# Slab pairs that take expert weights to the end, instead of turning into gather and result buffers

## The chip, the cores and the metric

The program runs on one core of a Trainium2 chip. The metric is device time in microseconds, the median of three runs. Beside it stands one profiled execution of the same program, whose rows carry all durations below.

## The reference

One transformer block on 1024 tokens of width 1024, in float32: a first half (projections, two kinds of attention, gates, an output projection) and a mixture of 32 experts, which is the stage that the change touches:

```
for e in range(N_EXPERTS):
    hidden = jax.nn.silu(t @ w_gate[e]) * (t @ w_up[e])
    out = out + combine[:, e:e + 1] * (hidden @ w_down[e]).astype(jnp.float32)
```

Each token goes to two of the 32 experts (the top two in its best group); `combine` is zero elsewhere. So 2048 token rows are computed in all, and the kernel gathers for each expert the rows that chose it, up to `BT` = 112 at a time.

## The kernel before, in words

The first 880 us or so are the block's first half and the router; the change leaves them alone. Then comes the stage of the experts, one expert after the other, e = 0 to 31.

An expert's weights are six slabs of 128x1024 floats (512 KB each): j = 0 to 3 hold gate and up, j = 4 and 5 hold down. A slab is loaded by SyncE (L870), then `split` (L82 to L84) makes two tiles of it for TensorE: ScalarE writes the rounded part `ehi`, VectorE writes the rest, `elo`. After both have read it, the slab is free and its next load may land. `weights(e, j0, j1)` (L1111) does this for a run of slabs and asks for the next loads in the order of `raw_order` (L860): expert by expert, j by j.

The raw slabs are 24 in number when the stage starts: five `er`, three `ex`, and 16 halves of eight pairs called `ring` (L125). The pairs held other things before (the input, then the merged branches) and are loaded with weights as they come free, while the router runs (`load_pairs`, L873). So experts 0 to 3 are in SBUF when the stage begins.

For each expert: `gather(e)` (L1129) fetches its token rows from the DRAM tensor `h2_d` by an indirect DMA that GpSimd issues; `tokens(e)` (L1135) turns them with eight TensorE transposes (L1139) and splits them to `xh` and `xl`; `gate_up(e)` (L1145), `hidden_t(e)` (L1159) and `down(e)` (L1169) compute; `down` writes a result buffer `y` (L1180 on ScalarE, L1182 on VectorE) and issues an indirect DMA on GpSimd that adds its rows to `out` (L1183, called a scatter below). A scatter waits until the one before it has landed, since two experts may add to one row.

A gather needs a free buffer of the list `gbuf`; it is free again once `tokens` has turned it. A `down` needs a buffer of `ybuf` whose last scatter has landed. Three of each (`g0` to `g2`, `y0` to `y2`) are there from the start. More come from the ring pairs: when both halves of a pair have been split, `weights` decides (L1121 to L1127). If fewer than `R_RAW` = 13 loaded slabs are waiting, the pair is loaded again; otherwise it becomes two gather buffers, until there are `GB` = 9, and after that two result buffers. With 24 slabs at the start the first five pairs turn: three into gather buffers (nine in all) and two into result buffers (seven in all), and 14 slabs stay for weights.

Engine queues run in order. GpSimd's holds the gathers and the scatters, SyncE's the loads. Where an instruction stands in its queue is set by the scheduler of the program's builder, not by the source alone. Experts' token turns come in pairs on TensorE: those of e+1 and e+2 stand side by side.

Of the kernel before, what the change touches and what calls it, by code (L numbers as in the profile page):

```python
# [28 lines left out]
NG, EPG, NE, FF = 4, 8, 32, 256  # L29
# [8 lines left out]
NYB = 3  # L38
N_MORE = 3
GB = 9  # L40
R_RAW = 13
LAGO = 1
LEAD = 16
FILL_M = 13.0 / 36
# [4 lines left out]
def kernel(ctx: ExitStack, tc: tile.TileContext, a, out):  # L49
# [32 lines left out]
    def split(hi, lo, src, eng=None):  # L82
        nc.scalar.activation(hi, src, AF.Copy)  # L83
        return (eng or nc.vector).tensor_tensor(lo, src, hi, op=ALU.subtract)  # L84
# [40 lines left out]
    def ring(dt):  # L125
        return pm.tile([P, 2, 1024], dt, name="ring", bufs=8)
# [5 lines left out]
    def er(i, dt=F32):  # L132
        return per.tile([P, 1024], dt, name=f"er{i % N_RAW}")
# [723 lines left out]
    psL = bank("o")  # L857

    RAW = {}
    raw_order = iter([(e, j) for e in range(NE) for j in range(6)])  # L860

    def load(unit):

        left = [len(unit)]
        for slab_ in unit:
            ej = next(raw_order, None)
            if ej is None:
                left[0] -= 1
                continue
            nc.sync.dma_start(slab_, a["w_exp"][ej[0], :, ej[1] * 1024:(ej[1] + 1) * 1024])  # L870
            RAW[ej] = (slab_, unit, left)

    def load_pairs(n):  # L873
        for _ in range(n):
            u = ring(F32)
            load([u[:, 0, :], u[:, 1, :]])
# [146 lines left out]
    for i in range(N_RAW):  # L1023
        load([er(i)])
    for i in range(N_MORE):
        load([pex.tile([P, 1024], F32, name=f"ex{i}")])
# [84 lines left out]
    def weights(e, j0, j1):  # L1111
        for j in range(j0, j1):
            raw, unit, left = RAW.pop((e, j))
            hi = pew.tile([P, 1024], F32R, name="ehi", bufs=7)
            lo = pew.tile([P, 1024], F32R, name="elo", bufs=7)
            split(hi, lo, raw)
            W[e, j] = (hi, lo)
            left[0] -= 1
            if left[0] or e == NE:
                continue  # L1120
            if len(unit) == 1:  # L1121
                load(unit)
            elif len(RAW) < R_RAW:
                load_pairs(1)
            else:
                u = ring(F32)
                (gbuf if len(gbuf) + len(gused) < GB else ybuf).extend([u[:, 0, :], u[:, 1, :]])  # L1127
# [72 lines left out]
    with tc.issue_after(acted.ins), tc.issue_after(listed.ins):  # L1200
        weights(0, 0, 6)
    tokens(0)
    for e in range(NE + 1):
        if e + 1 < NE:
            weights(e + 1, 0, 4)
# [5 lines left out]
        if e + 1 < NE:  # L1211
            weights(e + 1, 4, 6)
            turned = tokens(e + 1)
# [23 lines left out]
    with tc.For_i(0, nblocks, 1) as j:  # L1237
# [24 lines left out]
        for i in range(6):  # L1262
            RAW[NE, i] = (er(i), None, [1])
            nc.sync.dma_start(RAW[NE, i][0], src[:, i * 1024:(i + 1) * 1024])
            weights(NE, i, i + 1)
# [84 lines left out]
```

## Time and profile before

| | us |
|---|---|
| median of three runs (lowest, highest) | 1264.19 (1263.36, 1268.15) |
| the profiled execution's own time | 1264.64 |
| its span, first instruction to last | 1262.6 |
| TensorE busy | 1156.1 (92%) |
| VectorE busy | 945.8 (75%) |
| ScalarE busy | 746.8 (59%) |
| GpSimd busy | 188.7 (15%) |

The busy shares are means over stages with different limits. The stage of the experts runs from about 890 us to the end, and what a change in it is worth is read from its own windows. The DMA share of a window is the mean busy share of the core's 16 DMA engines. GpSimd's durations are rough; its starts are used here.

### The profile page before, as it was taken

How to read it: one execution, taken by the hardware profiler on the slowest of the kernel's cores; microseconds unless marked ns; L12 is line 12 of the kernel's file. 1: busy time of each engine (PE TensorE's matmuls, PEld its weight loads, DVE VectorE, ACT ScalarE, POOL GpSimd, SP SyncE). 2: the span in 40 equal slices, each digit the busy share in tenths (PEclk: the TensorE clock that was granted, in tenths of full speed). 3: DMA queues.
4: the chain of work that ended last, by engine and by line, in shares of the span. 5: the costliest groups of instructions: out<-in, count | busy, mean ns of one | idle time of the engine just before them, and what ended most of it. 6: DMA issues, size and time to landing. Idle time of an engine off the chain costs nothing. (4 is left out here: it accounts for less than half of the span.)

```text
span 1262.6 us, 18229 instructions
## 1 busy us (share of the span) xinstructions
PE 1156.1 (92%) x6105; PEld 944.6 (75%) x6105; DVE 945.8 (75%) x2099; ACT 746.8 (59%) x1400; POOL 188.7 (15%) x147
## 2 busy tenths in 40 slices
PE   7889999979999998999999999999499997988994
PEld 6778888868888886777787878788377775666773
DVE  4786783448888888888765776555699996878992
ACT  6544552347667677767664443322487885767882
POOL 1000000010000001111100000000256243632211
PEclk9999999989999999999999999999699999989998
DMA  7753355392332224432216345653779999999983
GB/s 272 218 182 101 127 163 158 110 203 76 100 92 76 69 83 117 126 93 75 67 59 217 132 135 215 220 188 134 255 232 344 308 319 301 317 306 330 359 307 54
DMA packets 107615, 228.62 MB, mean 181 GB/s; under 512 B 13984, under 2 KB 47392, under 8 KB 107520
## 3 DMA queue, kind: packets, MB, share of 16 engines
q1 hardware_dynamic: 81664, 193.59, 45.2%
q0 software_dynamic: 21248, 25.46, 9.6%
q10 hardware_dynamic: 4608, 8.39, 1.8%
q8 instruction: 49, 0.80, 0.3%
q14 instruction: 46, 0.38, 0.1%
HBM read 187.53 MB, written 52.43 MB: 190 GB/s over the span
## 5 line engine op out<-in xcount | busy, mean ns | idle before, releaser
L515 ACT ACTIVATE pd<-pA,nbd 128x512 f32<-128x512 f32 (+7 forms) x128 | 94.6, 740 | 38.7 <-DVE nbd L512 36.6
L84 DVE TENSOR_TENSOR elo<-ring,ehi 128x1024 fp32r<-128x1024 f32 x88 | 104.7, 1220 | 13.0 <-ACT ehi L83 12.9
L83 ACT ACTIVATE ehi<-ring 128x1024 fp32r<-128x1024 f32 x88 | 91.4, 1057 | 25.4 <-DMA ring<-in_w_exp 13.8
L87 PE MATMUL pG<-ring,whi 128*128 128x512 f32 x240 | 98.7, 411 | 6.5 <-ACT sg L489 6.5
L512 DVE TENSOR_REDUCE nbd<-pA 128x1 f32<-128x128 f32 (+7 forms) x128 | 95.6, 749 | 3.2 <-PE pA L563 2.2
L89 PE MATMUL pG<-ring,wlo 128*128 128x512 f32 x240 | 96.0, 400 | 0.1
L88 PE MATMUL pG<-ring,whi 128*128 128x512 f32 x240 | 96.0, 400 | 0.0
L84 DVE TENSOR_TENSOR elo<-er,ehi 128x1024 fp32r<-128x1024 f32 x65 | 76.9, 1220 | 11.8 <-ACT ehi L83 11.6
L83 ACT ACTIVATE ehi<-er 128x1024 fp32r<-128x1024 f32 x65 | 67.3, 1056 | 21.8 <-DMA er<-in_w_exp 12.5
L87 PE MATMUL pG<-ehi,xh 128*112 128x512 f32 x128 | 53.2, 416 | 19.3 <-ACT xh L83 19.2
L524 PE MATMUL pB<-ident,pd 128*128 128x128 f32 x432 | 66.3, 277 | 1.4 <-DVE pd L567 0.3
L87 PEld LDWEIGHTS pG<-ring,whi 128*128 128x128 f32 x240 | 45.9, 191 | 16.9 <-ACT sg L489 10.5
L524 PEld LDWEIGHTS pB<-ident,pd 128*128 128x128 f32 x432 | 49.1, 141 | 12.2 <-PE pO L591 2.6
L1183 POOL DMA_INDIRECT out<-ring,ids x17 | 38.0, 2238 | 116.0 <-DVE elo L84 39.6
L89 PE MATMUL pB<-ehi,ehl 128*112 128x512 f32 x128 | 53.2, 415 | 2.0 <-DVE ehl L84 2.0
L87 PE MATMUL pB<-ehi,ehh 128*112 128x512 f32 x128 | 53.3, 416 | 0.9 <-DVE y L1182 0.7
L87 PE MATMUL pO<-ehi,xh 128*112 128x512 f32 x128 | 52.0, 406 | 1.2 <-ACT ehi L83 1.1
L89 PEld LDWEIGHTS pG<-ring,wlo 128*128 128x128 f32 x240 | 45.9, 191 | 9.1 <-DVE wlo L84 0.3
L660 PE MATMUL pA<-x,x 128*128 128x512 f32 (+3 forms) x168 | 47.9, 370 | 5.0 <-ACT pd L515 4.8
L89 PE MATMUL pG<-ehi,xl 128*112 128x512 f32 x128 | 52.1, 407 | 0.0
L88 PE MATMUL pO<-elo,xh 128*112 128x512 f32 x128 | 50.4, 394 | 1.5 <-DVE elo L84 1.5
L88 PE MATMUL pB<-elo,ehh 128*112 128x512 f32 x128 | 51.7, 404 | 0.0
(395 smaller groups left out, 3567.5 us busy)
## 6 DMA issues: line engine op xcount, KB each, us to landing
ring<-in_w_exp SPq DMA_DIRECT2D x88, 512.0 KB
er<-in_w_exp SPq DMA_DIRECT2D x65, 512.0 KB
ex<-in_w_exp SPq DMA_DIRECT2D x39, 512.0 KB
er<-in_w_gate SPq DMA_DIRECT2D x16, 512.0 KB
g_d<-sg ACTq DMA_DIRECT2D x32, 256.0 KB
sgl<-g_d SPq DMA_DIRECT2D x32, 256.0 KB
er<-in_w_dqkv SPq DMA_DIRECT2D x8, 512.0 KB
xT<-in_xT SPq DMA_DIRECT2D x16, 256.0 KB
```

What stands on the lines that cost most here:

```text
L83: nc.scalar.activation(hi, src, AF.Copy)
L84: return (eng or nc.vector).tensor_tensor(lo, src, hi, op=ALU.subtract)
L87: nc.tensor.matmul(ps, ah, bh, start=start, stop=False)
L88: nc.tensor.matmul(ps, ah, bl, start=False, stop=False)
L89: nc.tensor.matmul(ps, al, bh, start=False, stop=stop)
L512: nc.vector.tensor_reduce(nb, ps[:, :n], axis=AX, op=ALU.max, negate=True)
L515: nc.scalar.activation(p[:, :n], ps[:, :n], AF.Exp, bias=nb, accum_out=s)
L524: nc.tensor.transpose(pt[:, (b - b0) * P:(b - b0 + 1) * P], p[:, b * P:(b + 1) * P], ident)
L660: nc.tensor.matmul(ps[f][:, k], q, ks[f][j][:, k], start=j == 0, stop=j == 1)
L1183: nc.gpsimd.indirect_dma_start(out=out[:, :], out_offset=bass.IndirectOffsetOnAxis(ap=idx[:BT, :], axis=0), in_=y[:BT, :], in_offset=None, ...
```

## The change

A pair whose halves have been split is loaded again as long as any of the 192 slabs has not been asked for. A set `loaded` counts them, and `R_RAW` is gone. Only when all 192 have been asked for do pairs go to `gbuf` and `ybuf`.

```
     RAW = {}
+    loaded = set()
     raw_order = iter([(e, j) for e in range(NE) for j in range(6)])
...
             RAW[ej] = (slab_, unit, left)
+            loaded.add(ej)
...
             if len(unit) == 1:
                 load(unit)
-            elif len(RAW) < R_RAW:
+            elif len(loaded) < 6 * NE:
                 load_pairs(1)
             else:
                 u = ring(F32)
                 (gbuf if len(gbuf) + len(gused) < GB else ybuf).extend([u[:, 0, :], u[:, 1, :]])
```

Weights then have 24 slabs up to the end instead of 14; gathers have three buffers instead of nine, and results three instead of seven, until the last four experts. Lines of the changed kernel stand one lower above L858 and one higher below L872.

SyncE's queue from the second load of `er0` on (the load of expert 4's first slab), before. `ring_10432` and its like are pairs, with the builder's numbers.

```order
L870 DMA er0_8991<-in_w_exp 128x1024
L870 DMA er1_8993<-in_w_exp 128x1024
L870 DMA er2_8995<-in_w_exp 128x1024
L870 DMA er3_8997<-in_w_exp 128x1024
L870 DMA er4_8999<-in_w_exp 128x1024
L870 DMA ex0_9001<-in_w_exp 128x1024
L870 DMA ex1_9003<-in_w_exp 128x1024
L870 DMA ex2_9005<-in_w_exp 128x1024
L870 DMA ring_10432<-in_w_exp 128x1024 x2
L870 DMA ring_10443<-in_w_exp 128x1024 x2
L870 DMA ring_10493<-in_w_exp 128x1024 x2
L870 DMA ring_10674<-in_w_exp 128x1024 x2
```

The same queue now, from the load of `ex2` on:

```order
L870 DMA ex2_9005<-in_w_exp 128x1024
L870 DMA ring_10253<-in_w_exp 128x1024 x2
L870 DMA ring_10296<-in_w_exp 128x1024 x2
L870 DMA ring_10320<-in_w_exp 128x1024 x2
L870 DMA ring_10331<-in_w_exp 128x1024 x2
L870 DMA ring_10381<-in_w_exp 128x1024 x2
L870 DMA ring_10424<-in_w_exp 128x1024 x2
L870 DMA ring_10435<-in_w_exp 128x1024 x2
L870 DMA ring_10485<-in_w_exp 128x1024 x2
L870 DMA er0_8991<-in_w_exp 128x1024
```

Before, four pairs are loaded in this round, and the numbers 10253, 10300, 10322, 10331 and 10391 are gather and result buffers; now all eight pairs are loaded, in the order in which they are used up.

GpSimd's queue from the fifth gather on, before (`g` and `ring` on the left are gathers into a buffer, `out_0` on the left a scatter from one):

```order
L1131 DMA g1_10176<-h2_d_66,ids_10155 112x1024
L1131 DMA ring_10253<-h2_d_66,ids_10155 112x1024 x2
L1131 DMA ring_10300<-h2_d_66,ids_10155 112x1024 x2
L1131 DMA ring_10322<-h2_d_66,ids_10155 112x1024 x2
L1131 DMA g2_10177<-h2_d_66,ids_10155 112x1024
L1183 DMA out_0<-y0_10180,ids_10155 1024x1024
L1131 DMA g0_9007<-h2_d_66,ids_10155 112x1024
L1183 DMA out_0<-y1_10181,ids_10155 1024x1024
```

The same queue now, from the fifth gather on:

```order
L1132 DMA g1_10176<-h2_d_66,ids_10155 112x1024
L1132 DMA g2_10177<-h2_d_66,ids_10155 112x1024
L1132 DMA g0_9007<-h2_d_66,ids_10155 112x1024
L1184 DMA out_0<-y0_10180,ids_10155 1024x1024
L1184 DMA out_0<-y1_10181,ids_10155 1024x1024
L1132 DMA g1_10176<-h2_d_66,ids_10155 112x1024
L1132 DMA g2_10177<-h2_d_66,ids_10155 112x1024
L1184 DMA out_0<-y2_10182,ids_10155 1024x1024
L1184 DMA out_0<-y0_10180,ids_10155 1024x1024
L1132 DMA g0_9007<-h2_d_66,ids_10155 112x1024
L1132 DMA g1_10176<-h2_d_66,ids_10155 112x1024
L1184 DMA out_0<-y1_10181,ids_10155 1024x1024
```

Before, twelve gathers (experts 0 to 11) stand ahead of the first scatter; now seven do, and from there on two scatters and two gathers alternate: gathers 9 and 10 stand behind scatter 3, gathers 11 and 12 behind scatter 5. The order of TensorE's, VectorE's and ScalarE's instructions in this stage is the same but for a few swaps of neighbours.

## Rows read from the trace of the kernel before

**Rows 1.** Busy time by stretch: window, length, engines (instructions), TensorE's clock, DMA share, GB/s.
```profile
940.00:1040.00 100.00, 97.39 (x475) 73.05 (x474) 96.20 (x125) 82.91 (x103) 43.08 (x19) 1.00 0.95 323
1040.00:1140.00 100.00, 84.02 (x381) 61.83 (x379) 76.16 (x81) 65.30 (x81) 42.70 (x18) 0.93 0.95 309
1140.00:1220.00 80.00, 74.82 (x362) 56.34 (x361) 74.30 (x81) 65.55 (x81) 18.27 (x9) 1.00 0.99 344
```

**Rows 2.** Waits from 905 us on: who waited for whom, total us, times, longest.
```profile
ACT ehi L83 <- DMA ring<-in_w_exp: 13.8, 13, 2.2
ACT ehi L83 <- DMA er<-in_w_exp: 12.5, 8, 2.9
```

**Rows 3.** Busy time of the stage's first 24 us, columns as in rows 1.
```profile
908.00:932.00 24.00, 23.63 (x106) 17.36 (x105) 17.95 (x19) 18.24 (x22) 13.16 (x8) 0.91 0.53 167
```

**Rows 4.** Timeline of SyncE's loads: start, length of the run, line, out<-in, count.
```profile
900.63 14.33 SPq L870 DMA_DIRECT2D ex<-in_w_exp  x3
929.54 8.38 SPq L870 DMA_DIRECT2D ring<-in_w_exp  x8
```

**Rows 5.** Timeline of VectorE: splits of ring slabs, and results of experts 0, 5, 10, 31.
```profile
916.26 1.23 DVE L84 TENSOR_TENSOR elo<-ring,ehi 128x1024 fp32r<-128x1024 f32 x1 [0.15 <-ACT ehi L83]
918.90 5.76 DVE L84 TENSOR_TENSOR elo<-ring,ehi 128x1024 fp32r<-128x1024 f32 x5 [0.53 <-ACT ehi L83]
927.63 0.75 DVE L1182 TENSOR_SCALAR y<-pB,wsl 112x512 f32<-112x512 f32 x1 [0.34 <-PE pB L89]
928.30 6.95 DVE L84 TENSOR_TENSOR elo<-ring,ehi 128x1024 fp32r<-128x1024 f32 x6
980.86 0.74 DVE L1182 TENSOR_SCALAR ring<-pB,wsl 112x512 f32<-112x512 f32 x1
1025.02 0.75 DVE L1182 TENSOR_SCALAR ring<-pB,wsl 112x512 f32<-112x512 f32 x1 [0.32 <-PE pB L89]
1236.41 1.22 DVE L84 TENSOR_TENSOR elo<-ring,ehi 128x1024 fp32r<-128x1024 f32 x1
1245.43 0.75 DVE L1182 TENSOR_SCALAR ring<-pB,wsl 112x512 f32<-112x512 f32 x1 [2.90 <-PE pB L89]
```

**Rows 6.** Timeline of GpSimd: L1131 gathers, L1183 scatters (0, 4, 10, 14, 28, 31).
```profile
917.75 0.98 POOL L1131 DMA_INDIRECT ring<-h_d,ids  x1 [7.73 <-DVE elo L84]
928.41 6.51 POOL L1131 DMA_INDIRECT g<-h_d,ids  x1 [0.30 <-issue]
935.22 1.58 POOL L1183 DMA_INDIRECT out<-y,ids  x1 [0.30 <-issue]
983.16 2.10 POOL L1183 DMA_INDIRECT out<-ring,ids  x1 [5.38 <-DVE elo L84]
1044.64 1.52 POOL L1183 DMA_INDIRECT out<-ring,ids  x1 [1.66 <-ACT ring L1180]
1083.28 1.82 POOL L1183 DMA_INDIRECT out<-y,ids  x1 [0.39 <-issue]
1230.96 1.71 POOL L1183 DMA_INDIRECT out<-y,ids  x1 [7.68 <-DVE elo L84]
1250.29 1.46 POOL L1183 DMA_INDIRECT out<-ring,ids  x1 [5.02 <-DMA out<-y,ids]
```

**Rows 7.** Chain that ended last: the last load's landing, and scatter 28's (start, us).
```profile
1221.43 4.10 DMA ring<-in_w_exp
...
1230.96 5.83 DMA out<-y,ids
```

**Rows 8.** DMA queues: packets, MB, share of 16 engines; issues, last the median us to landing.
```profile
q0 software_dynamic: 21248, 25.46, 9.6%
...
g<-h_d,ids POOLq DMA_INDIRECT x13, 10.9
```

**Rows 9.** Timeline of TensorE: ends of the token turns of experts 3 and 11.
```profile
923.99 0.35 PE L1139 MATMUL pA<-ident,g 112*128 112x112 f32 x2
...
1001.68 0.93 PE L1139 MATMUL pA<-ident,g 112*128 112x112 f32 x8
```

## What is predicted for the changed kernel

> **What bounds the kernel now.** I read the busy time by stretch first, since the page's means mix stages. From 940 to 1040 us VectorE works 96.2 of 100 us; from 1040 to 1140 only 76.16, from 1140 to 1220 74.30 of 80 [rows 1]. So the stage of the experts first goes at VectorE's pace, loses some 20 us in the middle, and then goes at VectorE's pace again. The waits say what is missing there: ScalarE's split of a slab (L83) waits for the load of its slab, 13.8 us for ring slabs and 12.5 for `er` slabs [rows 2], and VectorE's split follows ScalarE's. The DMA engines are busy at 0.95 in both stretches [rows 1]. Weights come too slowly, though the DMA has hardly any room.
>
> It had room earlier. From 908 to 932 us its share is 0.53 at 167 GB/s [rows 3]: 0.47 x 24 = 11.3 us of all 16 engines unused, just ahead of the stretch where they are short. The queue of loads shows why: after the third `ex` load, whose run ends at 915 us, no load is issued until 929.54 [rows 4], because the first pairs used up have become gather buffers.
>
> The end of the program is a second chain. Scatters are serial: from scatter 4 at 983.16 to scatter 14 at 1083.28 ten periods take 100.1 us, 10.0 each; from 28 to 31, with few loads left, three take 1250.29 - 1230.96 = 19.3, 6.4 each [rows 6]. The result of expert 10 is complete at 1025.02 + 0.75 = 1025.8 [rows 5], and its scatter starts at 1044.64 [rows 6], 18.9 us later: scatters lag behind computing there. The last result is complete at 1246.2 [rows 5], the last scatter starts at 1250.3, and 12.3 us later the span ends at 1262.6.
>
> **Step 1, loads into the hole.** The first three pairs are now loaded again. Their second halves are split at 916.26 + 1.23 = 917.5 and, by the run of five splits of 1.15 us from 918.90, at about 921.2 and 923.5 [rows 5]; the fourth pair's at 929.5 is where loads resume today. So six slabs, 6 x 0.524 MB = 3.15 MB, go into the hole; at the 344 GB/s of the late stretch [rows 1] that is 9.1 us of DMA. Against it, gathers 7 to 11 leave it, for want of buffers, and come later. The gathers' and scatters' queue moved 25.46 MB in 9.6% of the span [rows 8], 121 us, or 4.76 us per MB; without 16 plain loads of 0.524 MB, 64 indirect DMAs share 17.1 MB, 0.267 MB each, 1.27 us each at that price and 0.78 at 344 GB/s. Five gathers are 3.9 to 6.4 us; I take 5. Net 4 us (2.7 to 5.2) of DMA work done earlier.
>
> **Step 2, more slabs in flight.** From about 945 us on, 24 slabs are loading or waiting instead of some 14. What of the missing 5% share from 940 to 1140 (10 us) comes back, no row shows: at least 0, if the gaps are uneven engines, at most 10. I take 5. The last load, issued at 1221.43 and landed 4.10 us later, 1225.5 [rows 7], then lands about 9 us earlier, at 1217 (1210 to 1223).
>
> **Step 3, VectorE follows.** Today the last slab is split at 1237.6 [rows 5], 12 us after it has landed, since VectorE never makes up what it lost in the middle. It could finish no earlier than 1237.6 less its excess idle time: (23.8 - 3.8) + (5.7 - 3.0) = 22.7 us [rows 1], so 1215. With the last landing at 1217 and a split of ScalarE and VectorE of some 2.5 us, it is about 1221, 16 us earlier. The last result comes 8.6 us after the last split today, so at 1230 (1224 to 1240).
>
> **Step 4, the scatters.** Result 0 is complete at 927.63 + 0.75 = 928.4 [rows 5]; its scatter starts at 935.22, because the twelfth gather, at 928.41, holds GpSimd for 6.51 us [rows 6]. Now seven gathers stand ahead, and the last of them has its buffer by 924.3, when expert 3's token turn ends [rows 9]; scatter 0 starts at 928.7 (to 935). The first four periods took 983.16 - 935.22 = 47.9 us, 12.0 each, the next ten 10.0; I take 11.0 for the first four, 10.0 for 24, and 6.4 for the last three: 928.7 + 44 + 240 + 19.3 = 1232. The chain of results (1230) and this one are close to each other, and each stalls the other here and there: I add 3 us and put the last scatter at 1235.
>
> **Step 5, gathers just in time.** Gather 11 now stands behind scatter 5. Its rows are turned at 1001.68 [rows 9], 20.1 us after result 5 was complete (981.6) [rows 5]. Of these go 1.8 us for the scatter's issue, 0.3 to the next issue and 10.9 from issue to landing [rows 8], so 7.1 us are left, less the scatter's lag. A lag over 7 us makes every second token turn late, and VectorE's `xl` and all splits behind it in its queue wait. But a later turn makes later results, which cuts the lag: computing then goes at the scatters' period, which step 4 already has. The three result buffers bite later: `down` needs the scatter three before it landed, 3 x 10.0 less 9, a lag of about 20. Cost beyond step 4: taken as 0 (0 to 10).
>
> **The rest** costs nothing: no instruction is added, the engines' order stays, and the pairs' late turn into buffers needs no work. SyncE's read of the block count stands after load 61 now, whose buffer is free at the same time.
>
> **The sum.** Last scatter 1235, and the same 12.3 us to the end: span 1247.3. The profiled execution's own time is 2.0 us over its span, and 0.4 over the median of the runs: 1247.3 + 2.0 - 0.4 = 1249 us, 15 less than 1264.2.
>
> **Rivals.** *The DMA was the bound all along* (same). The share of 0.95 is already full for this mix of loads, gathers and scatters; then only step 1's net counts, the starved stretch moves later by what the six slabs cover, and the end comes 2.7 to 5.2 us earlier: 1259 to 1262, 1260. For it: the share. Against it: the late stretch reaches 0.99 and 344 GB/s, and the 12 us between last landing and last split.
>
> *The scatters get slower* (slower than before). A scatter's period is 6.4 us alone and 10.0 with some 14 slabs queued [rows 6]; if that grows with the depth of the queue, (10.0 - 6.4)/14 = 0.26 us per slab, 24 slabs make it 12.6. Three gather buffers chain computing to it. Then the last scatter is at 928.7 + 28 x 12.6 + 19.3 = 1301, the time 1315; at half that growth, 11.3, it is 1264.4 + 14 = 1278. It decides from a period of (1250.3 - 928.7 - 19.3)/28 = 10.8 us on, below which the program is faster. For it: the first four periods of 12.0 and their lone gathers. Against it: the ten of 10.0 came with a pair of gathers in every second period, as all do now.
>
> The Trainium skill, "DMA: Bandwidth & Descriptors", Queues, rings and completion order, says that each DMA engine goes round-robin between the queues that have work, a packet at a time. By that a deeper queue of loads does not lengthen a scatter once there is always a load behind it, and the sum stays at 1249; by a strict order of arrival it would be this rival. The trace agrees in part: 14 slabs ahead at 344 GB/s would be 21 us, and a gather lands in 10.9.
>
> *All of the lost time comes back* (faster still). If the last landing comes before 1213 and scatters keep to 9.5, VectorE's 1215 sets the end: 22.7 us less, 1241.5.
>
> **How the numbers follow.** Forecast (1242 to 1257) 0.60; the DMA bound 0.18; slower scatters 0.14; everything back 0.08. The range for 8 in 10 takes in the third rival and the first: 1240 to 1266. What a measurement can tell from no change is about 0.5%, 6.3 us: faster means below 1257.9, slower above 1270.5. Faster: 0.60 + 0.08 = 0.68; same: 0.18 and a little of the slower rival's near end, 0.19; slower 0.13.
>
> **What would show it.** Step 1: loads of ring slabs at about 917.5, 921 and 923.5, and a share above 0.8 from 918 to 932. Steps 2 and 3: VectorE's idle time between 1040 and 1140 below 12 us, last split near 1221. Step 4: scatter 0 near 929, periods of 10. Step 5: token turns that wait for their gathers, by no more than a few us each. The forecast is wrong if scatters' periods exceed 10.8, if VectorE is as idle as before but later, or if the last slab lands after 1223.

## The result, and the profile after

The changed kernel is slower: 1287.66 us, median of four runs (1282.67 to 1294.62), against 1264.39 for the kernel before beside them; the ratio of the runs is 1.016, 95% interval 1.0129 to 1.0191 (the two medians divided give 1.018). The profiled execution was the slowest of the four (1294.62 us, span 1292.8), some 7 us over the median.

Busy time by stretch, after, columns as in [rows 1]; the first line answers to [rows 3]:

```profile
908.00:932.00 24.00, 23.63 (x106) 17.37 (x106) 17.55 (x18) 17.84 (x22) 5.63 (x4) 0.90 0.79 258
940.00:1040.00 100.00, 91.85 (x435) 69.46 (x434) 89.02 (x116) 76.64 (x95) 44.62 (x17) 0.97 0.96 329
1040.00:1140.00 100.00, 85.76 (x388) 64.91 (x387) 78.74 (x86) 68.90 (x86) 38.83 (x19) 0.93 0.94 314
1140.00:1220.00 80.00, 67.06 (x303) 50.68 (x301) 62.28 (x68) 54.84 (x67) 28.33 (x13) 0.91 0.91 299
1220.00:1260.00 40.00, 36.31 (x168) 27.80 (x169) 32.86 (x36) 28.53 (x35) 17.12 (x5) 0.96 0.36 86
```

The hole is filled as meant: a DMA share of 0.79 instead of 0.53. But VectorE now idles in every stretch: 11 us from 940 to 1040 (3.8 before), 21.3 in the next 100 (23.8 before) and 17.7 in the 80 from 1140 on (5.7 before). The waits from 905 us on say for what, answering to [rows 2]:

```profile
ACT xh L82 <- PE pA L1140: 52.3, 12, 6.8
PEld pA L1140 <- DMA g<-h_d,ids: 41.4, 10, 5.4
DVE xl L83 <- ACT xh L82: 41.1, 12, 4.9
PE pA L1140 <- DMA g<-h_d,ids: 40.0, 11, 4.9
ACT ehi L82 <- DMA ring<-in_w_exp: 0.3, 1, 0.3
```

No split waits for weights any more (0.3 us). In their place token turns wait for their gathers, 40.0 us in 11 waits: the first, of 3.0 us, is that of expert 1, which waits in the kernel before too, and the other ten, from 1004 us on, are every second turn, for 2.9 to 4.9 us each. With them wait ScalarE's and VectorE's splits of the tokens.

Why a gather is late shows on GpSimd, here over one pair of experts; scatters (L1184) 14, 15 and 16 and gathers (L1132) 21 and 22 (start, duration, idle time before):

```profile
1097.86 1.52 POOL L1184 DMA_INDIRECT out<-y,ids  x1 [6.37 <-DVE ehd L1157]
1107.95 5.58 POOL L1184 DMA_INDIRECT out<-y,ids  x1 [8.56 <-DVE elo L83]
1113.83 1.03 POOL L1132 DMA_INDIRECT g<-h_d,ids  x1 [0.30 <-issue]
1115.16 1.01 POOL L1132 DMA_INDIRECT g<-h_d,ids  x1 [0.30 <-PE pB L88]
1122.18 1.52 POOL L1184 DMA_INDIRECT out<-y,ids  x1 [6.00 <-DVE ehl L83]
```

Scatter 14 holds GpSimd for 1.52 us, scatter 15 for 5.58. These are durations on GpSimd, which are rough, but the starts say the same: the next issue comes 5.88 us after scatter 15's start (1113.83 - 1107.95), and 1.80 us after that of a short scatter (1047.40 - 1045.60, in the rows of e7 below). VectorE at that time, and the two token turns on TensorE:

```profile
1106.40 6.94 DVE L83 TENSOR_TENSOR elo<-ring,ehi 128x1024 fp32r<-128x1024 f32 x6
1113.26 0.39 DVE L83 TENSOR_TENSOR ehl<-pB,ehh 128x224 fp32r<-128x224 f32 x1
...
1127.04 1.09 DVE L83 TENSOR_TENSOR xl<-pA,xh 128x896 fp32r<-128x896 f32 x1 [3.55 <-ACT xh L82]
```

```profile
1119.35 0.93 PE L1140 MATMUL pA<-ident,g 112*128 112x112 f32 x8
1124.33 1.73 PE L1140 MATMUL pA<-ident,g 112*128 112x112 f32 x8 [3.58 <-DMA g<-h_d,ids]
```

Scatter 15 starts inside a run of six `elo` splits without a gap (1106.40 to 1113.34) and ends at 1113.53, just behind it. What let it go seems to lie before the run's end, where VectorE had caught up with ScalarE (the run's last split, and ScalarE's `ehi` for it, which ends at 1112.08):

```profile
1112.12 1.23 DVE L83 TENSOR_TENSOR elo<-ring,ehi 128x1024 fp32r<-128x1024 f32 x1
```

```profile
1111.02 1.06 ACT L82 ACTIVATE ehi<-ring 128x1024 fp32r<-128x1024 f32 x1 [0.33 <-DVE elo L83]
```

The scatter ends 1.41 us after this split starts, about what a short scatter takes in all. Gather 21 stands behind it, is issued at 1113.83, and token turn 21 starts at 1124.33, 3.58 us late. Gather 22 wasn't late for its turn, 19 us further on. The late turn delays the results, which keeps computing in step with the scatters, and so the next odd scatter falls on the next run. A pair takes 1122.18 - 1097.86 = 24.3 us, 12.2 an expert. The size fits: 5.58 - 1.52 = 4.06 us more a pair is 2.0 an expert, and the period grew by 1.7, from 10.5 to 12.2 (table below). Every odd scatter from 5 to 27 takes over 3.5 us, 12 of 14 such ones in all, the others being 0 and 26; in the kernel before there are 4 of 32.

The chain that ended last has this loop in it (start, us, what):

```profile
1137.84 10.71 DMA g<-h_d,ids
1148.60 1.75 PE pA L1140 x8
...
1155.87 14.17 DMA out<-y,ids
1170.87 9.19 DMA out<-y,ids
...
1187.57 10.54 DMA g<-h_d,ids
```

The short scatter (1170.87) lands in 9.19 us, the long one before it in 14.17. The last three scatters start 6.4 to 6.8 us apart and the last at 1280.38, 30 us later than in [rows 6]:

```profile
1274.02 1.46 POOL L1184 DMA_INDIRECT out<-y,ids  x1 [5.31 <-DMA out<-y,ids]
1280.38 1.46 POOL L1184 DMA_INDIRECT out<-ring,ids  x1 [4.90 <-DMA out<-y,ids]
```

### The profile page after: what moved, and what is told of

Its sections match the earlier page's. It is cut to its first block, busy times and chain, and to the rows that moved or that the text cites. A ratio compares the mean times of both kernels' runs of the same rounds, so it can differ in the third digit from the quotient of the medians.

```text
span 1292.8 us, 18220 instructions
## 1 busy us (share of the span) xinstructions
PE 1164.9 (90%) x6105; PEld 954.2 (74%) x6105; DVE 945.6 (73%) x2099; ACT 747.6 (58%) x1400; POOL 203.3 (16%) x147
## 5 line engine op out<-in xcount | busy, mean ns | idle before, releaser
L83 DVE TENSOR_TENSOR elo<-ring,ehi 128x1024 fp32r<-128x1024 f32 x128 | 151.6, 1221 | 4.1 <-ACT ehi L82 4.1
L82 ACT ACTIVATE ehi<-ring 128x1024 fp32r<-128x1024 f32 x128 | 133.1, 1058 | 24.9 <-PE pO L88 15.2
L1184 POOL DMA_INDIRECT out<-y,ids x31 | 102.4, 3303 | 202.1 <-DVE elo L83 68.8
L88 PE MATMUL pG<-ring,wlo 128*128 128x512 f32 x240 | 95.9, 400 | 0.1
L87 PE MATMUL pG<-ring,whi 128*128 128x512 f32 x240 | 95.9, 399 | 0.0
L1140 PE MATMUL pA<-ident,g 112*128 112x112 f32 x256 | 36.8, 296 | 49.9 <-DMA g<-h_d,ids 49.9
L1140 PEld LDWEIGHTS pA<-ident,g 112*128 112x128 f32 x256 | 31.6, 161 | 57.7 <-DMA g<-h_d,ids 41.4
L83 DVE TENSOR_TENSOR xl<-pA,xh 128x896 fp32r<-128x896 f32 x32 | 34.4, 1088 | 41.1 <-ACT xh L82 41.1
L82 ACT ACTIVATE xh<-pA 128x896 fp32r<-128x896 f32 x32 | 28.8, 915 | 52.3 <-PE pA L1140 52.3
L86 PEld LDWEIGHTS pG<-ring,whi 128*128 128x128 f32 x240 | 45.7, 191 | 17.1 <-ACT sg L488 10.7
L523 PEld LDWEIGHTS pB<-ident,pd 128*128 128x128 f32 x432 | 49.0, 141 | 12.2 <-PE pO L590 2.6
L1132 POOL DMA_INDIRECT g<-h_d,ids x32 | 47.5, 1483 | 36.8 <-PE pA L1140 17.6
L87 PE MATMUL pG<-elo,xh 128*112 128x512 f32 x128 | 52.7, 412 | 0.0
## 6 DMA issues: line engine op xcount, KB each, us to landing
er<-in_w_exp SPq DMA_DIRECT2D x40, 512.0 KB, 12.1
```

Source lines behind the costliest of these rows:

```text
L86: nc.tensor.matmul(ps, ah, bh, start=start, stop=False)
L87: nc.tensor.matmul(ps, ah, bl, start=False, stop=False)
L88: nc.tensor.matmul(ps, al, bh, start=False, stop=stop)
L523: nc.tensor.transpose(pt[:, (b - b0) * P:(b - b0 + 1) * P], p[:, b * P:(b + 1) * P], ident)
L1132: nc.gpsimd.indirect_dma_start(out=gused[e][:BT, :], out_offset=None, in_=h2_d[:, :], in_offset=bass.IndirectOffsetOnAxis(ap=idx[:BT, :], ...
L1140: nc.tensor.transpose(pt[:, k * P:k * P + BT], gbuf[-1][:BT, k * P:(k + 1) * P], ident[:BT, :BT])
```

## The experiments

All ratios are to the kernel before, run beside them on the same chip. Scatters 4 and 24 are the starts on GpSimd in the profiled execution; the period is their distance over 20. "Gathers" is what TensorE's token turns waited for them, "weights" what ScalarE's `ehi` splits waited for loads, both from 905 us on. The turns of experts 0 and 1 wait in every kernel, 9.3 to 10.5 and 1.8 to 3.4 us; the first of them falls behind 905 us in some kernels and not in others. Where "gathers" is under 14, it is these waits alone, but for one of 3.2 us in e6.

| kernel | ratio (95% interval) | scatters 4, 24: period | gathers | weights |
|---|---|---|---|---|
| before | 1 | 983.2, 1192.2: 10.5 | 2.9 | 27.1 |
| changed | 1.016 (1.0129 to 1.0191) | 976.9, 1221.1: 12.2 | 40.0 | 0.3 |
| e1: 9 gather, 3 result, 18 slabs | 1.000 (0.9981 to 1.0019) | 990.2, 1201.6: 10.6 | 13.2 | 29.1 |
| e2: 3 gather, 7 result, 20 slabs | 1.0201 (1.0169 to 1.0233) | 982.2, 1230.3: 12.4 | 52.9 | 0.6 |
| e3: 3 gather, 3 result, 14 slabs | 1.0125 (1.009 to 1.0159) | 979.0, 1215.3: 11.8 | 42.7 | 1.3 |
| e4: fewer `elo` splits | 0.9965 (0.9944 to 0.9987) | 978.4, 1184.4: 10.3 | 12.3 | 45.1 |
| e5: 5 gather, 3 result, 22 slabs | 1.000 (0.9979 to 1.002) | 977.1, 1188.9: 10.6 | 2.5 | 23.0 |
| e6: gathers a scatter earlier | 1.0033 (1.0017 to 1.005) | 983.3, 1194.6: 10.6 | 6.5 | 17.7 |
| e7: runs of splits cut | 1.0022 (1.0004 to 1.004) | 974.6, 1186.6: 10.6 | 3.0 | 28.2 |
| e8: e6 and e7 | 1.0006 (0.9992 to 1.0021) | 979.4, 1192.7: 10.7 | 3.1 | 30.9 |
| e9: e5, fewer bytes loaded | 0.9884 (0.9841 to 0.9927) | 981.6, 1188.4: 10.3 | 12.6 | 9.9 |
| e10: e5, two scatter chains | 0.9961 (0.9942 to 0.998) | (other order) | 12.1 | 35.4 |
| e11: e5 and e7 | 1.0009 (0.999 to 1.0028) | 974.0, 1188.2: 10.7 | 3.1 | 29.6 |
| e12: before, runs cut | 1.0019 (1.0002 to 1.0036) | 977.9, 1195.7: 10.9 | 12.2 | 35.7 |

Theory A is the loop just read; B says that three result buffers hold `down` back; C that the deeper queue of loads slows the scatters (the prediction's slower rival); D that the long scatters have a cause in the DMA itself.

**e1, e2: which buffers.** The first three (e1) or two (e2) pairs turn at once, as before the change:

```
-            elif len(loaded) < 6 * NE:
+            elif turned_pairs[0] >= N_CONV and len(loaded) < 6 * NE:
                 load_pairs(1)
             else:
+                turned_pairs[0] += 1
                 u = ring(F32)
```

> The first three pairs become gather buffers as in the kernel before (nine gather, three result buffers), then no pair turns until all weights are asked for (18 slabs). Theory A (three gather buffers put each gather just behind a scatter, so token turns are locked to the scatters, and the lock puts every second scatter at the start of VectorE's run of splits, where GpSimd is held 5 to 6 us): token turns stop waiting for gathers, scatter period falls from 12.2 to 10 to 10.8, time 1250 to 1268. Theory B (three result buffers hold `down` back): period stays near 12, time 1280 to 1295. Theory C (the deeper queue of loads slows the scatters): 18 slabs are a little under halfway from 14 to 24, period about 11, time 1268 to 1278.

> The first two pairs become result buffers (three gather, seven result buffers, 20 slabs), then no pair turns until all weights are asked for. Theory A (gather buffers): no help, token turns still wait for their gathers, period 11.8 to 12.4, time 1278 to 1295. Theory B (result buffers): period back to about 10, time 1250 to 1268. Theory C (depth of the load queue, 20 slabs): period 11.3 to 11.7, time 1272 to 1283.

e1 is back at the time of before, e2 isn't: gather buffers are what is missing. B falls.

**e3: the depth of the queue.** Five pairs are held idle, with a small read of each at the end:

```
+            elif len(idle) < N_IDLE:
+                idle.append(ring(F32))
+                nc.vector.memset(idle[-1][:, 0, 0:1], 0.0)
             elif len(loaded) < 6 * NE:
```

> Three gather and three result buffers as in the changed kernel, but the first five pairs are held idle: 14 slabs for weights as in the kernel before. Theory A: the gathers still stand just behind scatters, period 11.8 to 12.4, and the weights come late besides: time 1280 to 1300. Theory C (the deeper queue of loads slows the scatters): with 14 slabs the period is back at 10, time 1260 to 1270. Theory B: as A.

With the 14 slabs of before the period is 11.8 and the time 1.0125: C falls. Its interval overlaps that of the changed kernel, so the ten slabs between them are worth nothing that these runs can tell; the weights come in time with 14 as well (1.3 us), since computing waits for gathers.

**e4: fewer splits.** For slabs 1 and 2 of each expert there is no `elo`:

```
+            if j in (1, 2) and e < NE:
+                nc.scalar.activation(hi, raw, AF.Copy)
+                lo = hi
+            else:
+                split(hi, lo, raw)
```

> The changed kernel without VectorE's split of slabs 1 and 2 of each expert (their lower halves are left out, TensorE multiplies the upper half twice): VectorE's runs of splits become shorter, four at most, while buffers, gathers, scatters and loads stay. Theory A (a scatter that starts in a run of VectorE's splits is held until the run ends): the long scatters on GpSimd shrink from 4.7-6.4 us to under 4 us, and their period from 12.2 to 11.5 or less, time 1265 or less. Theory D (every second scatter is long for a reason of the DMA itself, VectorE's run is a coincidence): long scatters stay at 5 to 6 us and the period at 12, time 1280 to 1295.

Three long scatters are left of 14, and the period is 10.3. But the scheduler now put one gather behind each scatter instead of two behind every second, so this run alone doesn't tell the splits from the queue's order. The next three change one thing each.

**e5: two more gather buffers.** As e1, with one pair (`GB = 5`, `N_CONV = 1`).

> Only the first pair becomes two gather buffers (five gather, three result buffers), then no pair turns until all weights are asked for (22 slabs). If the number of gather buffers matters because a gather stands behind a scatter that runs late, two more buffers put each gather one pair of scatters (20 us) earlier than needed: no token turn waits, time 0.99 to 1.003 of the kernel before. If the six buffers beyond three matter in another way (nine are needed), time 1.008 to 1.016 of before.

1.000: with two more buffers no turn behind the first two waits for its gather.

**e6: the place in the queue.** Buffers as in the changed kernel; an odd expert's scatter is issued behind the gather seven experts further on, which stood behind it:

```
+            behind = LASTG.get(s_ + 7) if s_ % 2 else None
+            with tc.issue_after(behind) if behind is not None else nullcontext():
+                nc.gpsimd.indirect_dma_start(
...
```

> The changed kernel with its three gather and three result buffers, but on GpSimd's queue each pair of gathers stands ahead of the odd scatter behind which it stood (gathers 11 and 12 ahead of scatter 5, and so on). Theory A (the place behind a late scatter makes token turns late): waits of token turns for gathers fall from some 80 us to under 20, computing gets out of step with the scatters, period 10 to 11, time 0.995 to 1.007 of before. If only the number of buffers counts (a fetch is late whatever its place), the waits and the time stay: 1.012 to 1.02 of before.

The waits fall from 40.0 to 6.5 us and the time to 1.0033, with three gather buffers as before.

**e7: the runs of splits.** The queue's order stays; one short VectorE instruction that reads nothing stands behind every sixth split:

```
+            cut = split(hi, lo, raw)
...
+            if j == 5 and e < NE:
+                with tc.issue_after(cut.ins):
+                    nc.vector.memset(gap, 0.0)
```

> The changed kernel with 32 more VectorE instructions: a memset of a scratch tile (128x256, which reads nothing) behind the last `elo` split of each expert, so that VectorE's runs of five or six splits become runs of three. If GpSimd is held until the first VectorE instruction that does not read two SBUF tensors: the long scatters shrink from 4.7-6.4 us to under 4, the period of a pair from 24.4 to some 22, time 0.995 to 1.008 of before. If a gap of one short memset does not release it, or the runs are not the cause: the long scatters stay at 4.7 us and more, time 1.015 to 1.025 of before.

1.0022, with 32 instructions more. Scatter 0 shows the effect by itself. In the changed kernel, GpSimd, and then VectorE's run of six splits over it with the last of them by itself:

```profile
929.63 6.28 POOL L1184 DMA_INDIRECT out<-y,ids  x1 [3.58 <-ACT ehi L82]
```

```profile
928.71 6.95 DVE L83 TENSOR_TENSOR elo<-ring,ehi 128x1024 fp32r<-128x1024 f32 x6
...
934.44 1.23 DVE L83 TENSOR_TENSOR elo<-ring,ehi 128x1024 fp32r<-128x1024 f32 x1
```

In e7, GpSimd, and then VectorE around it:

```profile
930.43 4.00 POOL L1188 DMA_INDIRECT out<-y,ids  x1 [3.55 <-ACT ehi L82]
```

```profile
929.51 3.49 DVE L83 TENSOR_TENSOR elo<-ring,ehi 128x1024 fp32r<-128x1024 f32 x3
933.00 0.27 DVE L1122 MEMSET gap<- 128x256 f32 x1
933.18 3.43 DVE L83 TENSOR_TENSOR elo<-ring,ehi 128x1024 fp32r<-128x1024 f32 x3
936.53 0.38 DVE L83 TENSOR_TENSOR ehl<-pB,ehh 128x224 fp32r<-128x224 f32 x1
```

The scatter ends at 934.43, in the middle of the second half of the run and 1.43 us after the memset started; in the changed kernel it ended at 935.91, 1.47 us after the run's last split started. A gap of 0.27 us let it go. D falls. Later on the odd scatters of e7 no longer meet a run; a gather does, and it has time (GpSimd in e7; L1136 are gathers 17 and 18, between scatters 11 and 12):

```profile
1045.60 1.50 POOL L1188 DMA_INDIRECT out<-y,ids  x1 [8.10 <-DVE ehd L1161]
1047.40 1.03 POOL L1136 DMA_INDIRECT g<-h_d,ids  x1 [0.30 <-PE pB L88]
1048.74 4.17 POOL L1136 DMA_INDIRECT g<-h_d,ids  x1 [0.30 <-issue]
1055.24 1.79 POOL L1188 DMA_INDIRECT out<-y,ids  x1 [2.34 <-DVE elo L83]
```

So both halves of theory A are shown: either edit alone undoes most of the loss. Not every run of splits holds GpSimd, though. In e6 four pairs of gathers start in a run of six, and get through in 1.24 and 1.95 us; the first pair, and VectorE over it:

```profile
1047.74 1.24 POOL L1132 DMA_INDIRECT g<-h_d,ids  x1 [0.30 <-issue]
1049.29 1.95 POOL L1132 DMA_INDIRECT g<-h_d,ids  x1 [0.30 <-issue]
```

```profile
1046.86 6.94 DVE L83 TENSOR_TENSOR elo<-ring,ehi 128x1024 fp32r<-128x1024 f32 x6 [0.90 <-ACT ehi L82]
```

This run follows 0.90 us of idle time, those over scatters 0 and 15 follow other work of VectorE without a gap. That this is what sets them apart is likely, but no run tests it.

**e8: both edits.**

> The last two edits together (gathers ahead of the odd scatter, runs of splits cut). If both causes are right: period 9.8 to 10.3, no token turn late, time 0.985 to 0.998 of the kernel before. If one of them is wrong: as the better of the two alone.

1.0006: no better than either, and not the gain that was forecast. The forecast of both causes (0.985 to 0.998) is missed. No gather behind the first two is late any more, but weights are waited for again, 30.9 us; the next two runs ask what bounds such a kernel.

**e9, e10: the DMA or the chain of scatters.** Both start from e5:

```
+            n = 768 if len(unit) == 1 and ej[0] >= 6 else 1024
+            nc.sync.dma_start(slab_[:, :n], a["w_exp"][ej[0], :, ej[1] * 1024:ej[1] * 1024 + n])
```

> The kernel with five gather buffers (1.000 of before), but 56 of the 150 weight loads from expert 6 on (those into `er` and `ex` slabs) fetch 768 of 1024 columns: 7.3 MB less, at the loads' price there (72.9 us for 25.6 MB in 100 us) 21 us less DMA work. The columns left out keep an earlier expert's weights. If the DMA engines bound the kernels that are not held up by gathers: 0.984 to 0.992 of before. If the chain of scatters, one every 10.5 us, bounds them: 0.995 to 1.002, since no scatter is left out.

```
+        to = g_d.rearrange("b p s -> (b p) s") if e % 2 and e < NE else out
```

> The kernel with five gather buffers, but the odd experts' scatters add to another DRAM tensor, so that they wait only for the odd one before (the odd experts' results are left out of the output). Same bytes, same splits, same loads. If the serial chain of scatters bounds the kernels that are not held up by gathers: the last scatter starts 10 us earlier or more, 0.98 to 0.993 of before. If the DMA engines bound them: 0.995 to 1.002.

e9 is 1.2% faster (0.7 to 1.6), some 15 us for 21 us of DMA work. VectorE in e5 and in e9, the middle stretch of [rows 1]:

```profile
1040.00:1140.00 100.00, 90.42 (x419) 67.27 (x418) 84.39 (x91) 73.61 (x91) 40.31 (x19) 0.95 0.93 304
```

```profile
1040.00:1140.00 100.00, 97.51 (x475) 73.25 (x474) 95.68 (x103) 83.50 (x104) 35.66 (x22) 1.00 0.94 302
```

The DMA is as busy in both; with fewer bytes per slab VectorE works 95.7 us instead of 84.4. e10 gains 0.4% (0.2 to 0.6), which lies in the range given for the DMA as the bound, and waits 35.4 us for weights: the serial chain holds back a few us at most. In e10 20 of 32 scatters take over 3.5 us, and yet the kernel is not slower; that fits theory A, since no gather behind the first two is late there and a scatter waits only for the last but one.

**e11, e12: a version that beats both?**

> Five gather buffers, 22 slabs, and the memset behind the last `elo` split of each expert that cuts VectorE's runs. If the DMA engines bound every kernel whose token turns are not late: 0.996 to 1.002 of the kernel before, weights arriving as late as before. If the long scatters and gathers that are left (nine of over 3.5 us from 925 us on with five buffers) cost time on the chain that ends last: 0.988 to 0.996.

> The kernel before with the same 32 memsets. If VectorE's long runs cost only where a gather stands just behind a scatter, they cost nothing here, where nine gather buffers give slack: 0.998 to 1.004 of before. If the long scatters and gathers of the kernel before (nine of over 3.5 us) sit on its last chain: 0.988 to 0.997.

None does. e11 waits 29.6 us for weights, and in e12, where the gathers have slack, cutting the runs brings nothing, as theory A has it.

## Why the prediction was wrong, step by step

**Step 1, loads into the hole: right.** The first ring load starts at 917.9, the share from 918 to 932 us is 0.83 (above 0.8 was expected; 0.43 before), and no split waits for weights after it.

**Steps 2 and 3, more slabs in flight: wrong, and hidden.** In the changed kernel the last load starts at 1216.7, against 1221.4 before, but nothing comes of it, since computing waits for gathers. Where that wait is taken away (e5, e8, e11) the gain of 15 us isn't there either: 1.000 to 1.001. I took 5 of 10 us of missing DMA share as coming back; it went the other way. The DMA queues from 930 to 1220 us (packets, MB, share of 16 engines), before and then e5 with 22 slabs:

```profile
q1 hardware_dynamic: 22340, 81.38, 77.7%
q0 software_dynamic: 6184, 12.43, 18.2%
```

```profile
q1 hardware_dynamic: 21787, 79.31, 76.1%
q0 software_dynamic: 6597, 13.05, 18.9%
```

Loads and indirect DMAs (the two other queues have 0.3% in both) take 95.9% of these 290 us before and 95.0% in e5: the share didn't rise with the slabs but fell by 2.6 us' worth, about the net work that step 1 put ahead (2.7 to 5.2), while 0.62 MB more of gathers and scatters fell into the stretch. The last load starts no earlier for it, at 1222.7 in e5 and 1221.4 before. The first rival, "the DMA was the bound all along", is what the kernels without the late gathers show; it gave 1260, and even its 3 to 5 us are not seen. Its starved stretch moved later, as it said: VectorE's idle time from 1040 to 1140 is 15.6 us in e5 and 23.8 before, and from 1140 to 1220 it is 14.4 and 5.7 (e5):

```profile
1140.00:1220.00 80.00, 69.69 (x319) 51.66 (x318) 65.59 (x71) 57.15 (x70) 24.73 (x12) 0.94 0.98 328
```

The share by itself does not show a bound: in the changed kernel, where no split waits for a load, the two queues still take 93.8% of these 290 us:

```profile
q1 hardware_dynamic: 21742, 79.19, 76.7%
q0 software_dynamic: 6082, 11.90, 17.1%
```

What shows it is e9, which moves fewer bytes and is faster.

**Step 4, the scatters: the term that was mis-sized.** Scatter 0 started at 929.63 (928.7 forecast). The first four periods took 976.91 - 929.63 = 47.3 us (44), the last three 1280.38 - 1260.43 = 20.0 (19.3). The 24 between took 1260.43 - 976.91 = 283.5 us, 11.8 each, where 10.0 stood: 43.5 us, nearly the whole error of this execution, 1294.6 - 1249 = 45.6 (of the median, 1287.7 - 1249 = 38.7). Even without late gathers 10.0 is too short: e5 to e8 have 10.6 to 10.7, and the kernel before itself 10.5 over twenty periods; I had read ten of them. Those 24 x 0.6 = 14 us are about the gain that was forecast.

**Step 5, gathers just in time: the step that failed.** Its cost beyond step 4 was taken as 0; the runs show some 29 us, 24 periods of 11.8 instead of the 10.6 that stand without late gathers. It had the place (gather 11 behind scatter 5, 7.1 us of slack) and even the coupling: "computing then goes at the scatters' period". Then it priced the coupling at "0 (0 to 10)", with the period as a constant. The period depends on where in VectorE's cycle a scatter starts, and the coupling fixes just that. The rows shown had the sign of it: the twelfth gather's 6.51 us at 928.41 in [rows 6] stands over VectorE's run of six splits, 928.30 for 6.95 us, in [rows 5]. I used the 6.51 us for scatter 0's start alone, did not ask why it was so long, and took it as gone with the gather. Scatter 0 then took its place in front of the same run (6.28 us).

**The slower rival: right in its result, wrong in its cause.** It gave 12.6 as the period and 1315 us, or 11.3 and 1278, decided from 10.8 on; 12.2 was measured. But depth of the load queue, its mechanism, is refuted by e3 (14 slabs, 11.8), and the short scatters land in 9.19 us with 24 slabs queued. The Trainium skill's rule on queues taken in turn ("DMA: Bandwidth & Descriptors", Queues, rings and completion order), which the prediction set against this rival, agrees with both of these; it spoke against the mechanism, not against the danger.

## What to carry to other kernels

When a change takes slack from one queue, price what the queue's own instructions cost at the phase that the new coupling forces, not at their mean: look up every long instance in the trace of before and what ran beside it. More buffers in front of the DMA brought nothing here while it was the bound, and its share didn't tell whether it was (0.94 without a wait for loads, 0.95 to 0.96 with); leave bytes out to test that before spending buffers on it. And a long stretch of one engine's work that shuts out another could be cut here by a single short instruction.

## What the runs showed of the hardware

An indirect DMA's issue on GpSimd can be held by VectorE's `tensor_tensor` with two SBUF inputs, and not for one instruction only but over several that follow without a gap: 5.58 us beside a run of 6.94, 6.28 us for scatter 0, where a scatter takes about 1.5 us otherwise. A memset of 0.27 us in between released it (4.00 us). In all three cases the issue ended 1.41 to 1.47 us after VectorE's memset or, without one, after the start of the run's last split, ahead of which VectorE had caught up with ScalarE. The `ehl` split behind the run, which has one input in PSUM, starts only 0.27 us before scatter 15 ends, so it isn't what released it. Runs of the same length that followed idle time of VectorE did not hold the gathers in e6 (1.24 and 1.95 us); why is open.

The Trainium skill, "SBUF — State Buffer", Who interferes with whom, says that a VectorE instruction with two SBUF inputs contends with a GpSimd instruction that reads SBUF, "not with one that only writes it", and that `tensor_tensor` was not seen to stall DMA. Here it holds up the issue of an indirect DMA with row indices in SBUF, in the runs that followed other work without a gap; whether reading the indices or writing descriptors is what waits, no run here separates. The measurement decides.
